# A state recurrence that takes its context as a weighted sum, and k and q projected by pairs of heads

## Chip, cores and metric

The kernel runs on one core of one Trainium2 chip. The metric is device microseconds (us) from the first to the last instruction and what lies around them; lower is better. The engines are PE (TensorE, matmuls), PEld (its weight loads), DVE (VectorE), ACT (ScalarE), POOL (GpSimd) and SP (SyncE, which here issues almost all transfers). Each engine works through its own queue in program order.

## The reference, cut to what matters

One layer on 512 latent tokens and 256 context tokens of 1024 channels. Both streams are normalised and modulated to `h` and `hc`, and one projection gives u, q, k, v and two gates. Then:

```
# S5 branch, both directions, 32 groups x 64 complex states
uc, ul = u of context, u of latents
_, h0  = scan(a, B uc)             # only the last state of the context is used
h      = scan(a, B ul, start=h0)   # h[t] = a h[t-1] + B u[t]
y      = gelu(Re(C h) + d u);  ya = y * sigmoid(y @ w_glu)
# attention branch: 4 heads, 2 x 64 dims, rope on latent q and k
q, k = rope(q), concat(k_ctx, rope(k));  yb = diff_attention(q, k, v)
x = x + g * norm(merge(ya, yb, gates) @ w_out)
x = x + g2 * norm(mixture of 16 experts (1024 -> 2048 -> 1024, float32) of norm(x))
```

The context's own output is not wanted, so only its end state h0 matters.

## The kernel before, in words

**The order of the work.** The program is one long list written out by hand, in these stages: loads, normalisation and u; the matrices of the recurrence (`matrices`, `state_make`, `cp_make`); gates 0 to 7 with the convolution taps, with the recurrence woven in; v; `readout`; the GLU and its projection; k, then q; attention with gates 8 to 15; the output projection; routing; 16 experts, whose weights (402 MB) stream in as fast as room comes free.

**The recurrence.** The 768 tokens are cut into 96 chunks of 8 (32 of context, 64 of latents). `SR` holds one complex state per chunk and direction. `scan` walks over the chunks: each step is four DVE instructions on 64 columns that multiply the last state by the eighth power of a (`AR`, `AI`, from `PW[:, :, 8]`) and add the chunk's input. `steps(n)` issues n of the 95 steps at given places: 4 after each half of a gate, 10 after each of three parts of v, and the rest before `readout`, which needs them all. PE follows the weights of a gate: a high part made on ACT (`prep_gate`) and a low part on DVE (`lo`, put off into `due` and issued by `second_parts`).

**The matrices.** `matrices` is a generator of DVE work; `ahead(n)` advances it n pieces, between the pieces of h (`h_of`) and u (`u_some`). `cp_make` follows, 20 products of 1024 columns on DVE in all, and after it the first gates' low parts.

**k, q and the ropes.** The weights of k come in four parts of 256 rows and 512 columns, all four heads in each (`fetch`, `k_some`), so no head's k is ready before the fourth part. Then `ropes` projects q head by head and turns k and q: ACT copies the product (`raw`), DVE shuffles it, POOL multiplies by the sines, DVE multiplies by the cosines and adds, ACT and DVE split the sum into a high and a low part (`k_parts`, `q_parts`; of q, one low part in two is POOL's). `scores(0)` opens attention: its maximum (`nm`) is queued on DVE behind the ropes. Gate 9 uses the same PSUM bank as gate 8 and waits for the tanh of gate 8, which is queued on ACT behind the exponentials of `scores(0)`.

**Room.** Twenty tiles of 2048 columns go round in a queue `E`: `take` pops one, `give` returns it. The twelve U tiles become six large buffers for the experts' weights, the eight L tiles stay.

Of the kernel before, what the change touches and what calls it, by code (L numbers as in the profile page):

```python
# [33 lines left out]
def layer(ctx: ExitStack, tc: tile.TileContext, A, out):  # L34
# [12 lines left out]
    ctx.enter_context(tc.manual_schedule())  # L47


    E = deque("U6 L0 U0 U7 U10 U3 U11 L1 L2 L3 L4 U8 U1 U9 U5 L5 L6 L7 U4 U2".split())  # L50
    for k in range(12):
        up.tile([128, 2048], F32, name="place", tag=f"U{k}")
    tag_of, held = {}, {}
# [186 lines left out]
    def fetch(dst, c0, p):  # L240

        DMA.dma_start(out=dst.rearrange("p (k f) -> p k f", k=2),
                      in_=w_in[256 * p:256 * p + 256, c0:c0 + 512].rearrange("(k p) f -> p k f", p=128))

    def lo(eng, o, a, hi):
        eng.tensor_tensor(o, a, hi.bitcast(F32), op=OP.subtract)  # L246

    def parts(raw, eng):
# [8 lines left out]
        return t, [v.rearrange("p (k f) -> p k f", k=2) for v in (hi_, lo_)]  # L257

    PASSES = ((0, 0), (0, 1), (1, 0))

# [249 lines left out]
    def matrices(tl):  # L510
        for par in range(2):
            V.tensor_copy(LT[64 * par:64 * par + 64].rearrange("p q d k j -> p (q d) k j"),
                          tl[64 * par:64 * par + 64, 0:256].rearrange(
                              "p (q d k r j) -> p (q d) k r j", q=4, d=2, k=2, r=2)[:, :, :, par])
        V.memset(PW[:, 0, 0], 1.0)
        V.memset(PW[:, 1, 0], 0.0)
        V.tensor_copy(PW[:, :, 1], LT[:, 0:2].rearrange("p q d k j -> p q (d k j)"))
        yield
        for n in (1, 2, 4):
            b_re = PW[:, 0, n:n + 1, :].to_broadcast([128, n, 32])  # L520
            b_im = PW[:, 1, n:n + 1, :].to_broadcast([128, n, 32])
# [18 lines left out]
        yield  # L540
        for gh in range(2):
            for dr in range(2):
                yield from state_make(dr, gh)
# [55 lines left out]
    ahead(1)  # L599
    h_of(1, 2, 2)  # L600
    ada_half(1)
    ahead(2)
    u_some(range(2), 0)
    u_some(range(2), 1)
    ada_mod(1)
    wu.append(parts(wur[2], GP))
    h_of(0, 4, 1)
    ahead(2)
# [128 lines left out]
    for dr in range(2):  # L737
        for gh in range(2):
            cp_make(dr, gh)
        second_parts()  # L740
    give(mm)
    BZ_ = take("BZ")
    BZ = BZ_.rearrange("p (r g a h) -> p r g a h", r=2, g=32, a=2)
    GP.memset(BZ_, 0.0)
# [12 lines left out]
    def rows(s):  # L757
        cb = 97 + (31 - s if s < 32 else 127 - s)
        return SR[:, s:cb + 1:cb - s]

    def scan():
        for s in range(1, 96):
            if s == 32:
                V.tensor_copy(SR[:, 97 + 96], SR[:, 97])
            h0, h1 = rows(s - 1), rows(s)
            sp = keep.tile([128, 2, 2, 16], F32, name="sp", bufs=2)
            sq = keep.tile([128, 2, 2, 16], F32, name="sq", bufs=2)
# [63 lines left out]
                    DMA.dma_start(out=MT[par][16 * s:16 * s + 16, :, 0:s], in_=KS[1][16 * par:16 * par + 16, :, 7 - s:7])  # L831

    ft = taps()
    wv = []
# [172 lines left out]
    DMA.dma_start(out=cosT, in_=A["rope_cos"])  # L1007
    DMA.dma_start(out=sinT, in_=A["rope_sin"])
    for p in range(2):
        fetch(kraw[p], 1024, p)  # L1010
    kw = []
    for n in range(8):
        pq = bank("proj")
# [2 lines left out]
        if n < 4:  # L1016
            prep_proj(n + 4, GP)
        if n in (4, 6):
            kw.append(parts(kraw[len(kw)], GP))
            fetch(kraw[len(kw) - 1], 1024, len(kw) + 1)  # L1020
    load_proj(8)
    give(*ya_, *PW_["t"])
    three[0] = False
# [28 lines left out]
    def q_parts(h, a):  # L1052
# [25 lines left out]
    wqs = []  # L1078

    def k_some(p, w, acc, hx):  # L1080
        for h in range(HEADS):
            for kt in (2 * p, 2 * p + 1):
                for n, (a, b) in enumerate(PASSES):
                    PE.matmul(acc[h], w[a][:, kt % 2, 128 * h:128 * h + 128], hx[b][kt],  # L1084
                              start=kt == 0 and n == 0, stop=kt == 7 and n == 2, skip_group_check=True)

    for p in range(4):
        t, w = kw.pop(0)
        if p < 2:
            kw.append(parts(kraw[p], GP))  # L1090
            fetch(kraw[p], 512, p)
        else:
            wqs.append(parts(kraw[p - 2], GP))
            fetch(kraw[p - 2], 512, p)
        k_some(p, w, kcc, hc)
        if p == 3:
            wqs.append(parts(kraw[0], GP))
            for h in range(HEADS):
                for _ in k_parts(h, slice(0, TC), kcc[h]):
                    pass  # L1100
        k_some(p, w, kacc, hh)
        give(t)
    give(*hc_)

    def rope_k(h):
        return rope(kacc[h], lambda a: k_parts(h, lat, a))
# [1 line left out]
    def rope_q(h):  # L1108
        pl = four[h]("q")
        for kt in range(8):  # L1110
            for n, (a, b) in enumerate(PASSES):
                PE.matmul(pl, wqs[kt // 2][1][a][:, kt % 2, 128 * h:128 * h + 128], hh[b][kt],
                          start=kt == 0 and n == 0, stop=kt == 7 and n == 2)
        return rope(pl, lambda a: q_parts(h, a))

    def ropes():

        live = []
        todo = deque(((rope_k, 0), (rope_k, 1), (rope_q, 0), (rope_k, 2), (rope_k, 3), (rope_q, 1), (rope_q, 2), (rope_q, 3)))
        while todo or live:  # L1120
            if todo:
                f, h = todo.popleft()
                live.append(f(h))
            for g in reversed(list(live)):
                if next(g, live) is live:
                    live.remove(g)
            yield

    fr = ropes()
    next(fr)  # L1130
    wqs.append(parts(kraw[1], GP))
    next(fr)
    gate_room(px_[:, 0:2048])
    load_gate(8)
    for n in range(2, 9):
        next(fr)
        if n == 4:
            prep_gate(8, GP)
        if n == 7:
            prep_gate(9, GP)  # L1140
    fq = fr
    give(*(t for t, _ in wqs))


    araw = [take("araw") for _ in range(2)]
# [737 lines left out]
```

## Time and profile before

| | |
|---|---|
| runs | 1590.41, 1594.12, 1594.39 us; median 1594.12 |
| the profiled execution | 1590.99 us, of which the span 1589.2 |
| busy share of the span | PE 87%, DVE 34%, ACT 18%, POOL 9% |
| HBM traffic | 461.66 MB read, mean 292 GB/s over the span |
| mean granted clock of TensorE | 0.954 |

Busy shares are means over unlike stages. Up to about 640 us stages are bound now by one engine, now by another; from then on the experts' weights stream in at about 427 GB/s.

### The profile page before, as it was taken

To read this page: it belongs to the slowest core of one execution; us is meant where nothing else is said; L and a number is where in the kernel's file an instruction comes from. 1 tells how busy PE (TensorE), PEld (TensorE's weight loads), DVE (VectorE), ACT (ScalarE), POOL (GpSimd) and SP (SyncE) were. 2 spreads that over 40 slices of the span, in tenths; PEclk is the share of its full clock that TensorE was granted. 3 is DMA by queue.
4 is the path that set the end of the run, shared out by engine and by line. 5 is a ranking of instruction groups with operands and counts; after the bars stand their busy time and mean duration, and the time that the engine had idled before them with its cause. 6 is when DMAs were issued, how large, how long until landed. Compare 5 with 4: busy or idle time off the path is not lost.

```text
span 1589.2 us, 17706 instructions
## 1 busy us (share of the span) xinstructions
PE 1388.3 (87%) x7230; PEld 748.7 (47%) x7230; DVE 540.4 (34%) x1373; ACT 291.7 (18%) x568; POOL 143.3 (9%) x103
## 2 busy tenths in 40 slices
PE   6996979996997896899999989879989989979875
PEld 3775757885664675434334324324324324324322
DVE  5798652267556646211102012002112112101103
ACT  3571204245433322100000000000000000000002
POOL 2100002453114200000000000000000000000003
PEclk9998989998997897899999999999999999999998
DMA  9110512222453156799999999999999999999994
GB/s 330 43 54 27 108 52 97 80 91 72 163 205 122 53 186 247 313 428 425 408 424 427 426 427 427 426 428 426 427 427 427 426 427 427 427 427 427 427 411 158
DMA packets 76737, 467.01 MB, mean 294 GB/s; under 512 B 13700, under 2 KB 33344, under 8 KB 46416
## 3 DMA queue, kind: packets, MB, share of 16 engines
q1 hardware_dynamic: 75472, 463.62, 72.5%
q10 hardware_dynamic: 768, 2.13, 0.4%
q8 instruction: 57, 0.93, 0.2%
q14 instruction: 24, 0.20, 0.0%
q0 software_dynamic: 416, 0.12, 0.0%
HBM read 461.66 MB, written 2.10 MB: 292 GB/s over the span
## 4 chain that ended last, share of the span: by engine, by line
PE 53%; DMA 23%; DVE 12%; ACT 2%; SPq 2%; issue 1%; POOL 0%; DVEq 0%; ACTq 0%
PE gu L1708 14%; DMA we<-in_w_exp_up_dram 13%; PE yd L1740 9%; DMA we<-in_w_exp_down_dram 9%; PE gat L1678 5%; PE gate L689 4%; PE sca L1752 4%; PE wo L1550 3%; PE k L1084 1%; PE proj L689 1%; PE y L907 1%; PE o L1260 1%; PE s L1222 1%; PE ada L1167 1%; PE K L812 1%
## 5 line engine op out<-in xcount | busy, mean ns | idle before, releaser
L1708 PE MATMUL gu<-we,gm 128*64 128x512 f32 x752 | 167.0, 595 | 18.2 <-DMA we<-in_w_exp_up_dram 10.3
L1708 PE MATMUL gu<-we,gf 128*64 128x512 f32 x752 | 167.9, 599 | 14.4 <-DMA we<-in_w_exp_up_dram 9.5
L1719 DVE TENSOR_TENSOR hid<-hid,gu 128x512 f32<-128x512 f32 x32 | 22.0, 688 | 461.0 <-PE gu L1708 461.0
L1740 PE MATMUL yd<-we,hid 128*64 128x512 f32 x688 | 152.3, 594 | 6.8 <-DMA we<-in_w_exp_down_dram 6.7
L689 PE MATMUL gate<-hh,wsp 128*128 128x512 f32 x384 | 99.3, 413 | 25.2 <-DVE wsp L246 12.8
L1708 PEld LDWEIGHTS gu<-we,gm 128*64 128x64 f32 x752 | 52.7, 137 | 131.0 <-issue 104.0
L1708 PEld LDWEIGHTS gu<-we,gf 128*64 128x64 f32 x752 | 53.2, 138 | 126.4 <-issue 103.3
L1793 POOL TENSOR_TENSOR fin<-facc,gf 128x256 f32<-128x256 f32 (+1 forms) x12 | 10.6, 910 | 997.9 <-DMA we<-in_w_exp_down_dram 993.7
L1740 PEld LDWEIGHTS yd<-we,hid 128*64 128x64 f32 x688 | 49.0, 137 | 102.9 <-issue 97.4
L689 PEld LDWEIGHTS gate<-hh,wsp 128*128 128x128 f32 x384 | 74.2, 199 | 42.9 <-DVE wsp L246 13.2
L1745 DVE COPY mo<-yd 64x512 f32<-64x512 f32 x15 | 10.4, 694 | 224.4 <-ACT mo L1744 224.4
L1678 PE MATMUL gat<-mo,x 128*128 128x128 f32 x512 | 76.5, 313 | 10.2 <-DVE mo L1670 10.2
L1678 PEld LDWEIGHTS gat<-mo,x 128*128 128x128 f32 x512 | 71.9, 221 | 18.3 <-issue 15.2
L1716 ACT ACTIVATE hid<-gu 128x512 f32<-128x512 f32 x32 | 19.1, 597 | 298.9 <-PE gu L1708 298.9
L1752 PE MATMUL sca<-mo,gm 128*128 128x512 f32 (+1 forms) x136 | 61.6, 591 | 4.8 <-ACT mo L1744 4.8
L1724 ACT COPY hid<-ht 128x512 f32<-128x512 f32 x16 | 9.4, 585 | 249.0 <-PE ht L1723 249.0
L1708 PE MATMUL gu<-wl,gm 128*64 128x512 f32 x208 | 48.5, 610 | 3.1 <-DMA wl<-in_w_exp_up_dram 3.1
L1744 ACT ACTIVATE mo<-yd 64x512 f32<-64x512 f32 x15 | 8.8, 589 | 215.9 <-PE yd L1740 215.9
L1550 PE MATMUL wo<-wo,mp 128*128 128x512 f32 x192 | 45.8, 394 | 2.3 <-DVE at L1410 2.3
L1757 DVE TENSOR_TENSOR facc<-facc,sca 128x512 f32<-128x512 f32 (+1 forms) x60 | 38.7, 652 | 18.8 <-PE sca L1752 18.7
L1740 PE MATMUL yd<-wl,hid 128*64 128x512 f32 x192 | 44.4, 596 | 0.0
L1752 PEld LDWEIGHTS sca<-mo,gm 128*128 128x128 f32 x136 | 21.5, 188 | 44.4 <-DVE facc L1757 23.6
(437 smaller groups left out, 1920.4 us busy)
## 6 DMA issues: line engine op xcount, KB each, us to landing
we<-in_w_exp_gate_dram SPq DMA_DIRECT2D x47, 2048.0 KB, 33.1
we<-in_w_exp_up_dram SPq DMA_DIRECT2D x47, 2048.0 KB, 29.7
we<-in_w_exp_down_dram SPq DMA_DIRECT2D x43, 2048.0 KB, 26.0
araw<-in_w_ada_dram SPq DMA_DIRECT2D x16, 1024.0 KB, 6.1
wl<-in_w_exp_gate_dram SPq DMA_DIRECT2D x8, 2048.0 KB, 29.3
wl<-in_w_exp_down_dram SPq DMA_DIRECT2D x8, 2048.0 KB, 31.3
wl<-in_w_exp_up_dram SPq DMA_DIRECT2D x8, 2048.0 KB, 26.9
wh<-in_w_exp_gate_dram SPq DMA_DIRECT2D x10, 1024.0 KB, 33.3
```

Of the source, the lines that this page charges most:

```text
L689: PE.matmul(ps, w[:, a, kt], x[b][kt], start=kt == 0 and n == 0, stop=kt == last and n == 2)
L812: PE.matmul(pkv[:, gi, j1:j1 + 7].rearrange("p t h -> p (t h)"), lh(dr, ri), CP[dr, ri][:, 128 * gp + 16 * dr:128 * gp + 16 * dr + 112], s ...
L907: PE.matmul(py[P, o0:o0 + 128], SR[P, r0:r0 + 64, ri, gp], CP[dr, ri][P, c0], start=False, stop=(dr == 1 and ri == 1), skip_group_check=True)
L1084: PE.matmul(acc[h], w[a][:, kt % 2, 128 * h:128 * h + 128], hx[b][kt], start=kt == 0 and n == 0, stop=kt == 7 and n == 2, skip_group_check ...
L1550: PE.matmul(po[j], mparts(a, kt)[:, 128 * i:128 * i + 128], wo[kt][:, D * b + 512 * j:D * b + 512 * j + 512].bitcast(F32R), start=kt == 0 ...
L1678: PE.matmul(pg, x1[i][:, nb(d)], oh[:, i].rearrange("p e s -> p (e s)"), start=i == 0, stop=i == 3)
L1708: PE.matmul(pq[b][64 * j:64 * j + 64], xst[e // 2 % 2][:, kt, e % 2], wv[:, c:c + 512], start=kt == 0, stop=kt == 7, skip_group_check=True)
L1716: S.activation(hid[0][:, 1 - e % 2, b], pq[b], AF.Silu)
L1719: V.tensor_tensor(act, act, pgu[1][b], op=OP.mult)
L1740: PE.matmul(py[64 * j:64 * j + 64], hT_[:, b, i, 64 * jf:64 * jf + 64], wv[:, c:c + 512], start=(q == 0 and i == 0), stop=(q == 3 and i == ...
L1752: PE.matmul(po, gm[:, g0:g0 + 128], yp_[:, ep % 2, c], start=True, stop=True)
L1757: V.tensor_tensor(dst, dst, po, op=OP.add)
```

## The change

**Context as a sum.** `matrices` gets six more pieces: `P8`, the powers 0 to 31 of the eighth power of a, by five complex products of 1, 2, 4, 8 and 15 powers. `context` forms the end state of the context of each direction as the sum over its 32 chunks of the chunk's input times a power: for the real and the imaginary part four products of 512 columns, one addition and one reduction of 1024 columns, all on DVE. It writes the sum into `SR`, and `scan` starts at step 32: 64 steps in place of 95.

**Where it stands.** Gates 0 and 1 have no steps beside them; after each, `second_parts` and one half of `context` follow. Gates 2 to 7 get 4 and 3 steps, each part of v gets 8. `mm` (scratch) and `P8` are given back after gate 1. The calls of `ahead` after the second half of the modulation are 4 and 1 in place of 2.

**k and q by pairs of heads.** A part of the weights is now 512 rows and 256 columns (two heads); after the second part heads 0 and 1 are complete, and their ropes run while the parts of heads 2 and 3 are projected. q of heads 0 and 1 needs only the first two parts of its weights. `launch` advances all ropes under way by one piece and starts another.

**Ropes.** The product with the sines and the second low part of q move from POOL to DVE.

**E** starts in another order.

```
@@ matrices
+        V.memset(P8[:, 0, 0], 1.0)
+        V.memset(P8[:, 1, 0], 0.0)
+        V.tensor_copy(P8[:, :, 1], PW[:, :, 8])
+        yield
+        for n in (1, 2, 4, 8, 16):
+            m = min(n, 31 - n)
...
+            cmul(V, P8[:, 0, n + 1:n + m + 1], P8[:, 1, n + 1:n + m + 1], P8[:, 0, 1:m + 1], P8[:, 1, 1:m + 1],
...
+            yield
@@ context, scan
+        for ri in range(2):
+            for d in range(2):
+                V.tensor_tensor(t[0][:, d], b[d][0], w[d][ri], op=OP.mult)
+                V.tensor_tensor(t[1][:, d], b[d][1], w[d][1 - ri], op=OP.mult)
+            V.tensor_tensor(t[0], t[0], t[1], op=OP.add if ri else OP.subtract)
+            V.tensor_reduce(ends[:, :, ri], t[0].rearrange("p d n g -> p d g n"), axis=AX.X, op=OP.add)
+            yield
+        V.tensor_copy(SR[:, 31], ends[:, 0])
+        V.tensor_copy(SR[:, 97::96], ends[:, 1:2].to_broadcast([128, 2, 2, 16]))
-        for s in range(1, 96):
-            if s == 32:
-                V.tensor_copy(SR[:, 97 + 96], SR[:, 97])
+        for s in range(32, 96):
@@ gates 0 to 7, v
-            steps(4)
-            if half == 0:
+            if n > 1:
+                steps(4 - half)
+            if half == 0 and n > 1:
                 second_parts()
...
+        if n < 2:
+            second_parts()
+            next(fctx)
+        if n == 1:
+            for _ in fctx:
+                pass
+            give(mm, P8_)
...
-        steps(5)
+        steps(8)
         second_parts()
-        steps(5)
@@ q_parts, rope
-            lo(V if c else GP, ql[h][PH[c]], a[PH[c]], qq[h][c][PH[c]])
+            lo(V, ql[h][PH[c]], a[PH[c]], qq[h][c][PH[c]])
-        GP.tensor_tensor(sw, sw, sinT, op=OP.mult)
-        yield
+        V.tensor_tensor(sw, sw, sinT, op=OP.mult)
@@ k, q
+    def launch(g):
+        advance()
+        next(g)
+        live.append(g)
...
+        k_some(p, w, kcc, hc)
+        if p % 2:
+            for h in (p - 1, p):
+                for _ in k_parts(h, slice(0, TC), kcc[h]):
+                    pass
+        if p == 3:
+            wqs.append(parts(kraw[0], GP, 4))
+        k_some(p, w, kacc, hh)
+        give(t)
+        if p % 2:
+            launch(rope_k(p - 1))
+            launch(rope_k(p))
+        else:
+            advance()
+            advance()
+    launch(rope_q(0))
+    wqs.append(parts(kraw[1], GP, 4))
     gate_room(px_[:, 0:2048])
     load_gate(8)
+    launch(rope_q(1))
+    prep_gate(8, GP)
+    launch(rope_q(2))
+    prep_gate(9, GP)
+    launch(rope_q(3))
```

## Rows read from the trace of the kernel before

**Rows 1.** The page's chain of work that ended last, shares by engine
```profile
PE 53%; DMA 23%; DVE 12%; ACT 2%; SPq 2%; issue 1%; POOL 0%; DVEq 0%; ACTq 0%
```

**Rows 2.** Busy time by stretch: us, engines' busy time, clock, DMA share, GB/s
```profile
120.00:140.00 20.00, 7.23 (x50) 5.55 (x49) 18.63 (x88) 1.54 (x2) 0.00 (x0) 0.66 0.00 1
340.00:360.00 20.00, 19.34 (x84) 15.02 (x83) 19.21 (x24) 10.98 (x18) 10.47 (x6) 1.00 0.46 151
920.00:1520.00 600.00, 541.81 (x2468) 209.87 (x2469) 86.28 (x191) 32.83 (x60) 0.00 (x0) 0.99 1.01 427
```

**Rows 3.** The chain in order of time, 130 to 235 us: start, us, what
```profile
132.80 1.23 DVE wsp L246
134.07 4.34 PE gate L689 x10
141.08 2.92 PE gate L689 x12
...
174.60 1.67 PE K L812 x16
...
196.66 4.67 DMA vraw<-in_w_in_dram
...
202.45 1.22 DVE wp L246
...
231.19 1.10 PE y L907 x16
```

**Rows 4.** One step's first instruction, L768: count, ns min/median/max, first and last start
```profile
L768 DVE TENSOR_TENSOR sp<-SR,AR x95: 218/224/342, 123.4 to 224.3; 128x64 f32<-128x64 f32 x95
```

**Rows 5.** Timeline of PE before the readout
```profile
207.22 5.60 PE L552 MATMUL v<-wp,hh 128*128 128x512 f32 x24
...
224.35 1.98 PE L907 MATMUL y<-CP,SR 64*64 64x128 f32 x16 [11.16 <-DVE SR L771]
```

**Rows 6.** Timeline of DVE, 40 to 85 us
```profile
42.58 0.29 DVE L430 TENSOR_TENSOR PW<-mm 128x128 f32<-128x128 f32 x1
...
66.48 3.17 DVE L456 TENSOR_TENSOR mm<-cn,PW 128x896 f32<-128x896 f32 x1
...
82.98 2.37 DVE L567 STREAM_TRANSPOSE u<-U 128x1024 f32<-128x1024 f32 x2 [2.79 <-ACT U L566]
```

**Rows 7.** DVE's groups, shapes apart, 334 to 371 us: count, busy us, mean ns
```profile
L1071 DVE TENSOR_TENSOR px<-px 128x512 f32<-128x512 f32 x3 | 6.9, 2312 | 0.3
L1071 DVE TENSOR_TENSOR at<-at 128x512 f32<-128x512 f32 x4 | 5.7, 1413 | 1.5 <-POOL at L1068 1.2
L1070 DVE TENSOR_TENSOR at<-at,px 128x512 f32<-128x512 f32 x4 | 5.5, 1369 | 0.0
L246 DVE TENSOR_TENSOR kq<-at,kq 64x512 fp32r<-64x512 f32 x6 | 4.1, 686 | 0.2
L1067 DVE STREAM_SHUFFLE px<-px 128x512 f32<-128x512 f32 x4 | 3.0, 738 | 0.1
...
L1070 DVE TENSOR_TENSOR px<-px 128x512 f32<-128x512 f32 x3 | 2.0, 676 | 0.0
```

**Rows 8.** Timeline of all engines, 365 to 371 us
```profile
365.29 2.50 POOL L246 TENSOR_TENSOR wsp<-px,wsp 128x1024 fp32r<-128x1024 f32 x1 [3.01 <-ACT wsp L680]
365.70 2.64 DVE L1071 TENSOR_TENSOR px<-px 128x512 f32<-128x512 f32 x1
...
370.22 0.96 DVE L1224 TENSOR_REDUCE nm<-s 128x1 f32<-128x768 f32 x1
```

**Rows 9.** Timeline of PE, 357 to 485 us
```profile
357.46 5.73 PE L689 MATMUL gate<-hh,wsp 128*128 128x512 f32 x24
375.17 5.38 PE L689 MATMUL gate<-hh,wsp 128*128 128x512 f32 x12 [11.98 <-ACT sg L703]
...
479.38 1.09 PE L1244 MATMUL pd<-ident,px 128*128 128x128 f32 x4 [1.47 <-DVE px L1237]
480.12 4.22 PE L689 MATMUL gate<-hh,wsp 128*128 128x512 f32 x12
```

More of the change, by code (lines that the diff above doesn't have):

```diff
@@ L243, in fetch, with fetch_heads, parts @@
                       in_=w_in[256 * p:256 * p + 256, c0:c0 + 512].rearrange("(k p) f -> p k f", p=128))
+    def fetch_heads(dst, c0, i):
+        DMA.dma_start(out=dst.rearrange("p (k f) -> p k f", k=4),
+                      in_=w_in[512 * (i % 2):512 * (i % 2) + 512, c0 + 256 * (i // 2):c0 + 256 * (i // 2) + 256]
+                      .rearrange("(k p) f -> p k f", p=128))
     def lo(eng, o, a, hi):
         eng.tensor_tensor(o, a, hi.bitcast(F32), op=OP.subtract)
-    def parts(raw, eng):
+    def parts(raw, eng, k=2):
         t = take("wp")
@@ L540, in matrices @@
         yield
+        V.memset(P8[:, 0, 0], 1.0)
[4 more added lines that the diff above has]
+            m = min(n, 31 - n)
+            b_re = P8[:, 0, n:n + 1, :].to_broadcast([128, m, 32])
+            b_im = P8[:, 1, n:n + 1, :].to_broadcast([128, m, 32])
+            cmul(V, P8[:, 0, n + 1:n + m + 1], P8[:, 1, n + 1:n + m + 1], P8[:, 0, 1:m + 1], P8[:, 1, 1:m + 1],
+                 b_re, b_im, *(mm[:, 1024 * i:1024 * i + 32 * m].rearrange("p (n g) -> p n g", n=m) for i in range(2)))
+            yield
         for gh in range(2):
@@ L601, in layer @@
     ada_half(1)
-    ahead(2)
+    P8_ = take("P8")
+    P8 = P8_.rearrange("p (r n g) -> p r n g", r=2, n=32)
+    ahead(4)
     u_some(range(2), 0)
@@ L605, in layer @@
     ada_mod(1)
+    ahead(1)
     wu.append(parts(wur[2], GP))
@@ L759, in rows, with context @@
         return SR[:, s:cb + 1:cb - s]
+    def context():
+        pw = [P8[:, ri].rearrange("p n (d g) -> p d n g", d=2) for ri in range(2)]
+        b = [[SR[:, 97 * d:97 * d + 32, ri] for ri in range(2)] for d in range(2)]
+        w = [[pw[ri][:, d, ::-1] if d == 0 else pw[ri][:, d] for ri in range(2)] for d in range(2)]
+        t = [mm[:, 1024 * i:1024 * i + 1024].rearrange("p (d n g) -> p d n g", d=2, n=32) for i in range(2)]
+        for ri in range(2):
[7 more added lines that the diff above has]
+        V.tensor_copy(SR[:, 97::96], ends[:, 1:2].to_broadcast([128, 2, 2, 16]))
+    ends = keep.tile([128, 2, 2, 16], F32, name="ends")
     def scan():
-        for s in range(1, 96):
-            if s == 32:
-                V.tensor_copy(SR[:, 97 + 96], SR[:, 97])
+        for s in range(32, 96):
             h0, h1 = rows(s - 1), rows(s)
@@ L1018, in layer @@
         if n in (4, 6):
-            kw.append(parts(kraw[len(kw)], GP))
-            fetch(kraw[len(kw) - 1], 1024, len(kw) + 1)
+            kw.append(parts(kraw[len(kw)], GP, 4))
+            fetch_heads(kraw[len(kw) - 1], 1024, len(kw) + 1)
     load_proj(8)
@@ L1080, in k_some, with advance @@
     def k_some(p, w, acc, hx):
-        for h in range(HEADS):
-            for kt in (2 * p, 2 * p + 1):
+        for h in (2 * (p // 2), 2 * (p // 2) + 1):
+            for k in range(4):
+                kt = 4 * (p % 2) + k
                 for n, (a, b) in enumerate(PASSES):
-                    PE.matmul(acc[h], w[a][:, kt % 2, 128 * h:128 * h + 128], hx[b][kt],
+                    PE.matmul(acc[h], w[a][:, k, 128 * (h % 2):128 * (h % 2) + 128], hx[b][kt],
                               start=kt == 0 and n == 0, stop=kt == 7 and n == 2, skip_group_check=True)
[L1087 to L1103, printed above, removed]
+    live = []
+    def advance():
+        for g in list(live):
+            if next(g, live) is live:
+                live.remove(g)
+    def launch(g):
+        advance()
+        next(g)
+        live.append(g)
     def rope_k(h):
@@ L1111, in rope_q, with ropes_left @@
             for n, (a, b) in enumerate(PASSES):
-                PE.matmul(pl, wqs[kt // 2][1][a][:, kt % 2, 128 * h:128 * h + 128], hh[b][kt],
+                PE.matmul(pl, wqs[2 * (h // 2) + kt // 4][1][a][:, kt % 4, 128 * (h % 2):128 * (h % 2) + 128], hh[b][kt],
                           start=kt == 0 and n == 0, stop=kt == 7 and n == 2)
         return rope(pl, lambda a: q_parts(h, a))
[L1116 to L1132, printed above, removed]
+    for p in range(4):
+        t, w = kw.pop(0)
+        if p < 2:
+            kw.append(parts(kraw[p], GP, 4))
+            fetch_heads(kraw[p], 512, p)
+        else:
+            wqs.append(parts(kraw[p - 2], GP, 4))
+            fetch_heads(kraw[p - 2], 512, p)
+        k_some(p, w, kcc, hc)
[10 more added lines that the diff above has]
+            launch(rope_k(p))
+        else:
+            advance()
+            advance()
+    give(*hc_)
+    launch(rope_q(0))
+    wqs.append(parts(kraw[1], GP, 4))
     gate_room(px_[:, 0:2048])
     load_gate(8)
[L1135 to L1141, printed above, removed]
-    give(*(t for t, _ in wqs))
+    launch(rope_q(1))
[3 more added lines that the diff above has]
+    launch(rope_q(3))
+    give(*(t for t, _ in wqs))
+    def ropes_left():
+        while live:
+            advance()
+            yield
+    fq = ropes_left()
     araw = [take("araw") for _ in range(2)]
```

8 lines of the change are left out of this document (4 added, 4 removed).

## The prediction

> **What bounds the kernel now.** I read four views, from far to near. First the shares of the chain that ended last: PE 53%, DMA 23%, DVE 12% [rows 1]. DVE is busy for a third of the span, yet an eighth of the chain is its own, so in some stages it is the late one. Second, the stretches show where. From 920 to 1520 us the DMA share is 1.01 at 427 GB/s: there the experts' weights set the pace, and nothing of this change works there. In 120 to 140 us DVE is busy for 18.63 of 20 us and PE for 7.23, at a mean granted clock of 0.66; in 340 to 360 us DVE is at 19.21 and POOL at 10.47 [rows 2]. Third, the chain in order of time and PE's timeline say what PE waits for. Gate 2 starts at 134.07, right behind a low part that DVE made at 132.80 [rows 3]. The readout starts at 224.35 after 11.16 us of idle PE, released by the last step of the recurrence [rows 5]. Gate 9 starts at 375.17 after 11.98 us, released by the tanh of gate 8 [rows 9]; that stood on ACT behind exponentials, which waited for the maximum that DVE began only at 370.22 [rows 8]. So PE has three holes, all made by DVE's queue. Since the weights stream into room that PE's work frees, I let all that is won before 375 us move the end by as much.
>
> **The change, part by part. Less work on DVE?** Hardly. Thirty-one steps go. Twelve steps stand between their first instruction at 123.4 and 132.80 [rows 3, 4], 0.79 us each, so 24.5 us go. In their place come the powers and the sum. A product of 128 columns takes 0.29 us, one of 512 columns 0.69 [rows 6, 7]; in proportion 32, 64, 256 and 480 columns take 0.19, 0.22, 0.42 and 0.65. Five complex products of six instructions: 6 x (0.19 + 0.22 + 0.29 + 0.42 + 0.65) = 10.6, with two memsets and a copy 10.8 us. The sum: eight products at 0.69, two additions of 1024 columns at 1.22 (as the low part at 202.45 [rows 3]), two reductions at 0.96 x 1024/768 = 1.28 [rows 8], copies 0.4: 10.9 us. DVE saves 24.5 - 21.7 = 2.8 us. What counts is where the work lies.
>
> **The powers, 54 to 95 us.** DVE has slack before the transposes at 82.98: the largest gap is the 2.79 us just before them [rows 6]. But six pieces more at the same number of `ahead` calls push three products of `state_make` behind the transposes, 3 x 1.1 us (896 columns in proportion to the 1.22) = 3.3, and from there to gate 2 I found no gap on DVE's timeline. And the product at 66.48 took 3.17 us where 1.1 is its own time [rows 6], so DVE is held up while it should catch up; with fuller queues I add 1.9. The low part for gates 0 and 1 and the products of `cp_make` are queued behind, and PE waits for both. I take 5.2 us; bounds 3.3 (the rest hidden) and 10.8 (nothing hidden).
>
> **Gate 2.** Before, twelve steps (9.35 us) stand between the last product of `cp_make` and the low part for gate 2. Now none does: it starts at 123.4 + 5.2 = 128.6 and PE's gate at 129.9, against 134.07: 4.2 us won. The sum's first half (5.4), the low part of gate 3 and the second half are queued behind; gate 3's is done at 136.6, and PE wants it at 129.9 + 11.2. From there to the end of the taps PE is the bound: 174.60 + 1.67 = 176.27 before [rows 3], 172.1 now. SP's 30 small transfers follow, then those of v's third and fourth part: 196.66 before, 192.5 now.
>
> **The readout.** By then 42 + 8 steps are issued, and DVE has had 50 us for them. What is left is a queue on DVE: v's third low part, which waits for the transfer (202.45 - 4.2 = 198.2, ending 199.5), eight steps (6.3), the fourth low part (1.2), six steps (4.7): 211.7. PE is free earlier, since v ends at 207.22 + 5.60 = 212.8 before [rows 5] and 208.6 now. So the readout starts at 211.7 against 224.35: **12.6 us**. Bounds: 2.8 (DVE the bound all the way, so that only its own saving counts) and 14.5 (only 3.3 us lost to the powers). Work moved past SP's queue costs nothing here: the loads keep their places.
>
> **k, q and the ropes.** PE's products stay as they are in number and size, so I leave gate 8 in its place (357.46 to 363.2 [rows 9]). DVE's work by head is a shuffle 0.74, three products or sums at 0.68 and two low parts at 0.69 [rows 7]: 4.2 us, where two heads' worth now runs under the projections of heads 2 and 3. Of the seven last ropes' sums and products, three groups took 10.7 us more than 11 x 0.68 [rows 7]: one began at 365.70 while POOL worked from 365.29 to 367.79 and ended 0.55 us after it [rows 8]. With the sines on DVE (8 x 0.68 + 4 x 0.69 = 8.2 us more) most of these meetings go; POOL keeps the low parts of weights. The maximum then needs the scores, which end before 357.46 (the first half about 1 us earlier, at 356.6), and behind q2's rope I allow for one meeting with POOL, 2.5 us [rows 8]: it starts at 359.1. From maximum to gate 9 it took 375.17 - 370.22 = 4.95 us; so gate 9 starts at 364.1, hardly later than gate 8 and its tanh allow (363.2 + 0.6). **11.1 us.** Bounds: 11.4, and 3 if DVE stays the late one (below). Gate 8's weights are loaded in time if q's last part, now converted behind the first q, doesn't hold them up; its wait would stand on ACT, ahead of q's copies.
>
> The Trainium skill (Perfetto Trace Analysis, Optimizing Scalar/DVE Operations) speaks against this edit: with a saturated VectorE, giving work to ScalarE or even GpSimd may make sense, and here it is taken back. The same skill (SBUF — State Buffer, Who interferes with whom) holds that a VectorE instruction with two SBUF inputs and a GpSimd instruction that reads SBUF exclude each other, the later one blocking fully, which is what the 2.64 us at 365.70 shows. By the first alone the edit costs 8.2 us, by the second it gives back more than it costs; the row decides for the second.
>
> **The clock.** After each hole PE runs slow at first: gate 2's first 10 records took 4.34 us against 2.92 for 12 [rows 3], gate 9's 12 took 5.38 [rows 9], the readout's first groups 1.98 against 1.10 [rows 3, 5]: about 1.4 + 2.5 + 2 = 5.9 us. Holes of 1 to 4 us remain, and after one of 1.47 us 12 records took 4.22 [rows 9]. Half is won: **3 us**, bounds 0 and 5.9.
>
> **Sum:** 1591.0 - 12.6 - 11.1 - 3.0 = 1564.3 us for the profiled execution. The median of the runs shown lies 3.1 us above it; I forecast 1565.
>
> **The rivals.** *DVE is the bound from 54 to 224 us* (the powers are paid in full, on a queue whose work shrinks by 2.8 us). For it: 18.63 of 20 us before 140; against it: PE alone is busy throughout 141 to 176. Readout 2.8 us early, little of the clock: 1591 - 2.8 - 11.1 - 1.5 = 1576. Chance 0.12.
>
> *DVE stays late in the ropes*: the long instructions are not POOL's doing, or the new meetings with its low parts cost as much, so that 11.1 less 8.2 = 3 us is left: 1591 - 12.6 - 3 - 1.5 = 1574. For it: 19.21 of 20 us. Chance 0.12. It is what the first page named above would give.
>
> *The change buys nothing*: the holes are filled, and the time is lost again before the experts begin, as where attention is paced by DVE's short waits. For it: 12% of the chain is DVE's in many places. Within 0.3% of 1594 us, about what a measurement of this kernel can tell from no change. Chance 0.04.
>
> *Slower: the experts' stream falters.* `E` starts in another order, so other tiles become the ring of buffers, and SP takes room strictly in order: one piece freed late holds up all behind it. The share is 1.01 now [rows 2]. Over some 890 us of streaming a loss of 3% costs the 27 us won; at 5% it is 44.5: 1564 + 44.5 = 1609. Against it: in the listing the tiles that serve the last stages before the experts stay the same in kind. Chance 0.04.
>
> **Numbers.** Forecast 0.68, its own range 1557 to 1572 (low: powers 3.3, clock in full; high: no clock, powers 8). With the two weaker cases the range is 1555 to 1579; what is left out is the same, the slower and the tails, 0.2. Faster by over 0.3%: 0.68 + 0.24 = 0.92; within 0.3%: 0.04; slower: 0.04.
>
> **What would show it.** Right: gate 2 near 130, the readout near 212 and gate 9 near 350 (364 less the readout's gain and some clock), each behind a hole of under 4 us; DVE's sums in the ropes near 0.7 us; experts' stream at 427 GB/s, begun some 26 us earlier. Wrong: the first product of `cp_make` over 8 us later than now; the readout still waiting over 6 us for the last step; ACT idle before the weights of gate 8; a DMA share under 0.98 after 920 us less the shift.

## The result, and the profile after

The changed kernel takes 1575.28 us, median of four runs (1571.01 to 1577.86), beside 1594.26 before (1590.41 to 1595.14). The ratio of the runs is 0.9883, with a 95% interval of 0.9854 to 0.9912: 1.2% faster. The forecast was 1565, its range 1555 to 1579. The profiled execution is the fastest of the four, 1571.01 us, its span 1569.2 against 1589.2: 20.0 us less.

The page's chain of waits of the changed kernel, to be set beside [rows 1]:

```profile
PE 53%; DMA 24%; DVE 9%; ACT 3%; SPq 2%; issue 1%; POOL 0%; DVEq 0%; ACTq 0%
```

DVE's share of the chain has fallen by three points, though its busy time has gone from 540.4 to 542.1 us. Busy time by stretch, with the columns of [rows 2]:

```profile
120.00:140.00 20.00, 17.03 (x111) 13.81 (x110) 19.55 (x22) 5.22 (x7) 0.56 (x1) 1.00 0.17 53
340.00:360.00 20.00, 14.59 (x54) 10.97 (x53) 14.88 (x23) 16.21 (x25) 7.16 (x3) 0.85 0.30 116
920.00:1520.00 600.00, 539.87 (x2452) 207.49 (x2452) 84.61 (x185) 32.88 (x60) 0.00 (x0) 0.99 1.01 427
```

From 120 to 140 us DVE is still full, but PE now works 17 of the 20 us. The experts' stream is at 427 GB/s as before. PE's timeline of the changed kernel, 110 to 365 us:

```profile
118.86 11.63 PE L710 MATMUL gate<-hh,wsp 128*128 128x512 f32 x50 [0.48 <-ACT SR L755]
133.46 2.56 PE L710 MATMUL gate<-hh,wsp 128*128 128x512 f32 x10 [2.97 <-DVE wsp L252]
...
210.64 0.44 PE L944 MATMUL y<-MT,u 128*64 128x128 f32 x4
212.88 1.17 PE L951 MATMUL y<-CP,SR 64*64 64x128 f32 x16 [1.80 <-DVE SR L807]
...
344.58 5.73 PE L710 MATMUL gate<-hh,wsp 128*128 128x512 f32 x24
355.72 5.33 PE L710 MATMUL gate<-hh,wsp 128*128 128x512 f32 x12 [5.41 <-ACT sg L724]
```

The reader is to compare the brackets with [rows 3, 5, 9]. The hole before gate 2 is 2.97 us and was 12.77, the one before the readout 1.80 and was 11.16, the one before gate 9 5.41 and was 11.98. But gate 2 starts only 0.6 us earlier: its work now begins late instead, since gate 0 starts at 118.86 and not at 109.64. The 20.0 us of the profiled execution are: readout 11.5 earlier; 1.0 in the readout, which took 25.6 us from first to last product and takes 24.6; 7.0 between the readout's end and gate 9, 125.2 us before (249.93 to 375.17) and 118.3 now (237.45 to 355.72); 0.5 behind that.

### The profile page after: what moved, and what is told of

Read it like the earlier page. It is cut to its first block, busy times and chain, and to the rows that moved or that the text cites. A ratio compares the mean times of both kernels' runs of the same rounds, so it can differ in the third digit from the quotient of the medians.

```text
span 1569.2 us, 17614 instructions
## 1 busy us (share of the span) xinstructions
PE 1388.5 (88%) x7230; PEld 747.5 (48%) x7230; DVE 542.1 (35%) x1307; ACT 292.5 (19%) x568; POOL 125.4 (8%) x91
## 4 chain that ended last, share of the span: by engine, by line
PE 53%; DMA 24%; DVE 9%; ACT 3%; SPq 2%; issue 1%; POOL 0%; DVEq 0%; ACTq 0%
PE gu L1761 15%; DMA we<-in_w_exp_up_dram 13%; DMA we<-in_w_exp_down_dram 10%; PE yd L1793 10%; PE gat L1731 5%; PE gate L710 4%; PE sca L1805 4%; PE wo L1603 3%; PE k L1128 1%; PE proj L710 1%; PE o L1313 1%; PE y L951 1%; PE s L1275 1%; PE ada L1220 1%; PE K L848 1%
```

## The experiments

Times of one kernel spread over some 5 us from run to run, so what separates two kernels is read from distances in the profiles. Three are enough. *Front*: from the second block of products of `ada` (at 51.2 to 52.8 us) to gate 0. *Readout*: when its first product with the states starts, from the start of the span. *Ropes*: from the readout's last product to gate 9. Each ratio is to runs of the kernel before that were made beside that kernel (their medians are 1592.8 to 1594.3 us), so it is not the quotient of two medians of the table.

```
kernel        median   ratio to before [95%]        front  readout  ropes
before        1594.26  1                             58.4   224.35  125.2
changed       1575.28  0.9883 [0.9854, 0.9912]       67.4   212.88  118.3
ctx_only      1583.58  0.9949 [0.9934, 0.9964]       70.1   217.76  125.3
kq_only       1584.98  0.9961 [0.9948, 0.9975]       58.3   224.44  118.4
sines_pool    1587.02  0.9963 [0.9952, 0.9975]       70.0   217.29  120.7
load_first    1575.51  0.9896 [0.9876, 0.9917]       70.2   218.00  118.4
no_powers     1570.57  0.9850 [0.9830, 0.9869]       62.3   212.24  118.1
half_steps    1576.58  0.9889 [0.9867, 0.9910]       70.1   216.06  118.1
powers_late   1573.29  0.9887 [0.9861, 0.9913]       62.6   216.45  118.2
lows_dve      1579.32  0.9909 [0.9889, 0.9929]       70.4   218.88  116.2
pfront        1570.35  0.9853 [0.9835, 0.9870]       58.3   214.07  118.3
early_lows    1573.13  0.9868 [0.9845, 0.9891]       70.1   217.89  113.5
both          1567.56  0.9831 [0.9812, 0.9851]       58.3   212.92  113.4
both_v        1563.17  0.9821 [0.9799, 0.9843]       58.4   208.92  113.4
```

**The halves alone.** First Context's part with the old k, q and ropes, then the other way round; one line of each edit:

```
 ctx_only: the changed kernel, with k, q and the ropes of before
-        fetch_heads(kraw[p], 1024, p)
+        fetch(kraw[p], 1024, p)
 kq_only: the kernel before, with k, q and the ropes of the changed one
-        fetch(kraw[p], 1024, p)
+        fetch_heads(kraw[p], 1024, p)
```

> Only Context's part of the recurrence is changed (powers, weighted sum, 64 steps, the order of the tiles); k, q and the ropes are as before. Theory (the change's two halves add, and what is won before the readout is carried through): the readout starts 11.5 us earlier, near 212.9, k at 286.8, and gate 9 near 362.7, 12.5 us earlier than the 375.17 of before, again behind a hole of about 12 us; the time is 12 to 13 us below before, about 1582. Rival (as predicted, the ropes are worth 11.1 us and the rest of the loss lies in the front): the time is only 9 us below before, about 1585.

> Only k, q and the ropes are changed; the recurrence has its 95 steps and the tiles their old order. Theory (the ropes' share of the 20 us is 7 to 8, the same whatever comes ahead of them): the readout starts at 224.4 as before, gate 9 near 368, 7 us earlier than before, behind a hole of about 5 us released by the tanh of gate 8, with the copy of gate 8's weights on ACT waiting for their transfer; the time is 7 to 8 us below before, about 1587. Rival (the loss of 4 us against the predicted 11.1 comes from the earlier front, which shifts POOL's low parts against DVE's products): alone, the ropes give the predicted 11 us, about 1583.

Measured: ctx_only has the ropes of before (125.3); kq_only has the front and the readout of before and the ropes of the changed kernel (118.4), with gate 9 at 368.48 behind a hole of 5.51 us, as its theory has it (its time, 1585.0, lies between theory and rival). So the ropes' 7 us are their own. The front and the readout of ctx_only are not the 67.4 and 212.88 of the changed kernel's one profile, as its theory had them, but 70.1 and 217.76, as in the other kernels below that have the powers in the front. Of the 4.9 us between the readouts 1.0 lies ahead of the front and 2.7 in it, and gate 2's first 10 products cost 1.5 (4.09 us, not 2.56), of which a little is won back; why comes below. By the ratios the halves save 0.51% and 0.39%, some 8 and 6 us; the whole saves 1.17%, which the three intervals just allow. In the profile of ctx_only gate 9 starts 7.5 us earlier than before, not 12.5, and some of that is lost again later: in the projection behind attention a group that took 5.74 us before (562.45) takes 7.37 (555.71), at a mean granted clock of 0.77 where it was 1.00. That is not the old ropes' doing: load_first below, with the new ones, shows 7.34. The time of ctx_only, 1583.6, lies between the theory's figure and the rival's, and the rival's reason fails, since the ropes alone give 7 and not 11.

**Sines back on POOL.**

```
         V.stream_shuffle(sw, raw, swap)
-        V.tensor_tensor(sw, sw, sinT, op=OP.mult)
+        GP.tensor_tensor(sw, sw, sinT, op=OP.mult)
+        yield
...
-            lo(V, ql[h][PH[c]], a[PH[c]], qq[h][c][PH[c]])
+            lo(V if c else GP, ql[h][PH[c]], a[PH[c]], qq[h][c][PH[c]])
```

> As the changed kernel, but the ropes' products with the sines and one of q's two low parts are back on POOL, each with its extra stage of the pipeline, as before the change. Theory (DVE's products of two SBUF inputs are held up while POOL reads): DVE's products and sums in the ropes show instructions of over 1.2 us again, at least six of them, and gate 9 comes 3 to 7 us later; 1578 to 1582. Rival (work given to POOL is work off a busy DVE, 8 us of it): gate 9 comes at the same time or up to 5 us earlier; 1570 to 1575.

Timeline of all engines of this kernel, from 345 us:

```profile
345.30 1.74 POOL L1112 TENSOR_TENSOR at<-at,px 128x512 f32<-128x512 f32 x1
...
345.92 1.68 DVE L1114 TENSOR_TENSOR at<-at,px 128x512 f32<-128x512 f32 x1
347.00 2.79 POOL L252 TENSOR_TENSOR wsp<-px,wsp 128x1024 fp32r<-128x1024 f32 x1
347.70 2.64 DVE L1115 TENSOR_TENSOR at<-at 128x512 f32<-128x512 f32 x1
349.76 1.71 POOL L252 TENSOR_TENSOR kq<-at,qq 64x512 fp32r<-64x512 f32 x1
...
351.53 0.94 PE L1276 MATMUL s<-kq 64*128 64x512 f32 x2 [4.47 <-POOL kq L252]
```

In both pairs shown DVE's product ends some 0.55 us behind POOL's, so that here DVE waits out the work that was given to POOL; and the scores themselves now wait 4.47 us for POOL. Six sums and products of DVE take over 1.2 us from 305 us on, as the theory has it. Gate 9's first half starts 120.7 us behind the readout, 2.4 later than in the changed kernel, and its second half, at 376.10, 134.2 (125.9 in the changed kernel): 8.3 us later. The time, 1587.0, is above the theory's 1578 to 1582. How much of the 8.3 us is the meetings, how much POOL's own lateness and how much the extra stage isn't separated.

**Load of gate 8's weights first.** In the changed kernel's timeline three things stand out between q0 and gate 9:

```profile
330.73 1.06 ACT L258 ACTIVATE wp<-px 128x1024 fp32r<-128x1024 f32 x1
...
331.87 2.75 POOL L252 TENSOR_TENSOR wp<-px,wp 128x1024 fp32r<-128x1024 f32 x1 [10.16 <-ACT wp L258]
332.29 2.88 DVE L1113 TENSOR_TENSOR at<-at,px 128x512 f32<-128x512 f32 x1
334.65 0.37 SPq L691 DMA_DIRECT2D px<-in_w_in_dram  x1
...
340.32 1.06 ACT L701 ACTIVATE wsp<-px 128x1024 fp32r<-128x1024 f32 x1 [2.49 <-DMA px<-in_w_in_dram]
341.41 1.28 ACT L1101 ACTIVATE qq<-at 64x512 fp32r<-64x512 f32 x2
...
345.79 2.40 POOL L252 TENSOR_TENSOR wsp<-px,wsp 128x1024 fp32r<-128x1024 f32 x1 [1.94 <-ACT wsp L701]
345.94 2.79 DVE L1112 TENSOR_TENSOR px<-px 128x512 f32<-128x512 f32 x1
...
350.15 0.96 DVE L1277 TENSOR_REDUCE nm<-s 128x1 f32<-128x768 f32 x1
```

DVE's products meet POOL at 332.29 and 345.94 (2.8 us each where 0.69 is their own time), and ACT waits 2.49 us for a load that goes out only at 334.65: it fills the buffer that POOL's low part at 331.87 still reads. This experiment takes away the second:

```
-    launch(rope_q(0))
     wqs.append(parts(kraw[1], GP, 4))
     gate_room(px_[:, 0:2048])
     load_gate(8)
+    launch(rope_q(0))
```

> As the changed kernel, but the last part of q's weights is converted, and the load of gate 8's weights issued, ahead of the first head of q in the order of the program instead of behind it. Theory (the ropes gave 7 and not 11 us because ACT waits at 340.32 for that load, with q0's and q1's copies queued behind): the 2.49 us of idle ACT there and the 0.31 us of PE go, gate 9 starts 1.5 to 4 us earlier than 355.72, and the time is 1.5 to 4 us below the changed kernel's, 1571 to 1574. Rival (DVE's meetings with POOL alone make the ropes late): ACT's wait goes, and gate 9 stays within 0.5 us of 355.72; 1575.

Its timeline of all engines in the same stretch:

```profile
332.06 2.77 POOL L252 TENSOR_TENSOR wp<-px,wp 128x1024 fp32r<-128x1024 f32 x1 [5.25 <-ACT wp L258]
332.49 2.89 DVE L1113 TENSOR_TENSOR px<-px 128x512 f32<-128x512 f32 x1
...
342.99 1.06 ACT L701 ACTIVATE wsp<-px 128x1024 fp32r<-128x1024 f32 x1
344.13 2.77 POOL L252 TENSOR_TENSOR wsp<-px,wsp 128x1024 fp32r<-128x1024 f32 x1 [9.31 <-ACT wsp L701]
344.56 2.88 DVE L1113 TENSOR_TENSOR at<-at,px 128x512 f32<-128x512 f32 x1
```

ACT's bracket is gone, and the ropes still take 118.4: three products of DVE now meet POOL (332.49, 344.56, 351.71). My theory alone does not hold; gate 9's distance and the time are as the rival has them.

**POOL's low parts on DVE.** Now the meetings go instead. The low part of gate 9 was put behind the exponentials, which write over the weights that it reads: in this kernel gate 9's values are not the reference's, and that part waits for them.

```
-    wqs.append(parts(kraw[1], GP, 4))
+    wqs.append(parts(kraw[1], None, 4))
+    launch(rope_q(1))
+    second_parts()
     gate_room(px_[:, 0:2048])
     load_gate(8)
-    launch(rope_q(1))
-    prep_gate(8, GP)
+    prep_gate(8, None)
     launch(rope_q(2))
-    prep_gate(9, GP)
+    second_parts()
+    prep_gate(9, None)
...
         if i == 0:
+            second_parts()
```

> As the changed kernel, but three low parts of weights that POOL makes beside the ropes (the last of q, gates 8 and 9) are made by DVE instead, each at a place where its chain waits or behind the maximum. Theory (what is missing of the ropes' 11 us are DVE's three products of 2.8 us while POOL works): no product or sum of the ropes behind q0 takes over 1.2 us, the maximum starts 2 to 4 us earlier behind the readout, gate 9 too, and the time is 2 to 4 us below the changed kernel's, 1571 to 1573. Rival (the products' wait is replaced by DVE's own low parts at 1.2 us and by the waits for their transfers): gate 9 stays within 1 us of its distance of 142.9 us from the readout; 1574 to 1577.

Two rows of its timeline, SP's queue and ACT:

```profile
341.01 0.37 SPq L691 DMA_DIRECT2D px<-in_w_in_dram  x1
...
346.78 1.06 ACT L701 ACTIVATE wsp<-px 128x1024 fp32r<-128x1024 f32 x1 [5.04 <-DMA px<-in_w_in_dram]
```

Between q0 and gate 9 the meetings are gone and the ropes take 116.2, 2.1 us less, as the theory has it; but ACT's wait for the load has grown from 2.49 to 5.04 us. The time, 1579.3, is outside both ranges; its interval overlaps that of the changed kernel. The place of gate 9's part explains some of it: the gate's second half starts at 371.19, 7.8 us later than in the changed kernel, where the readout was 6.0 later, so there the 2.1 us are lost again.

**Both at once.**

```
             launch(rope_k(p - 1))
+            if p == 3:
+                wqs.append(parts(kraw[1], None, 4))
             launch(rope_k(p))
...
-    launch(rope_q(0))
-    wqs.append(parts(kraw[1], GP, 4))
+    second_parts()
     gate_room(px_[:, 0:2048])
     load_gate(8)
+    launch(rope_q(0))
     launch(rope_q(1))
-    prep_gate(8, GP)
+    prep_gate(8, None)
     launch(rope_q(2))
+    second_parts()
-    prep_gate(9, GP)
+    prep_gate(9, None)
     launch(rope_q(3))
+    second_parts()
```

> As the changed kernel, but the last part of q's weights is converted between the ropes of k2 and k3, the load of gate 8's weights is issued right behind it, and the low parts of these and of gates 8 and 9 are made by DVE instead of POOL, behind the sums of k3, q1 and q2. Theory (two things hold the ropes up in turn, DVE's meetings with POOL and ACT's wait for gate 8's load, and either is hidden behind the other when only one goes): no product of the ropes behind k3 takes over 1.2 us, ACT does not wait for the load, and gate 9 starts 139 to 140.5 us behind the readout against 142.8 (changed kernel) and 143.0 (load ahead alone); 2 to 4 us less time than the changed kernel, 1571 to 1573. Rival (the chain of each head from ACT to DVE and back sets the pace, and neither matters): gate 9 stays within 1 us of 142.8 behind the readout; 1574 to 1577.

The same places in its timeline, and PE's gate 9:

```profile
329.13 1.23 DVE L252 TENSOR_TENSOR wp<-px,wp 128x1024 fp32r<-128x1024 f32 x1 [0.17 <-ACT wp L258]
...
330.43 0.37 SPq L691 DMA_DIRECT2D px<-in_w_in_dram  x1
...
341.53 1.06 ACT L701 ACTIVATE wsp<-px 128x1024 fp32r<-128x1024 f32 x1
...
355.99 3.02 PE L710 MATMUL gate<-hh,wsp 128*128 128x512 f32 x12 [1.10 <-ACT sg L724]
```

The load goes out 4.4 us sooner than in load_first, ACT finds it there, no product of the ropes behind k3 takes over 0.69 us, and PE's hole before gate 9 is 1.10 us; the 12 products behind it take 3.02 us and not 5.33. The ropes take 113.5, 11.8 less than before the change. It is more than the theory claimed (138.1 us from readout to gate 9, where 139 to 140.5 was expected). The two causes had stood behind each other: with one of them left, nothing (load_first) or 2.1 us (lows_dve) is gained, with both gone 4.8. The median is only 2.2 us below the changed kernel's, and the intervals overlap, so this rests on the distances.

**The powers left out.**

```
         for n in (1, 2, 4, 8, 16):
-            cmul(V, P8[:, 0, n + 1:n + m + 1], ...)
             yield
...
-        pw = [P8[:, ri].rearrange("p n (d g) -> p d n g", d=2) for ri in range(2)]
+        pw = [P8[:, ri, 1:2].to_broadcast([128, 32, 32]).rearrange("p n (d g) -> p d n g", d=2) for ri in range(2)]
```

> The 30 products that make the powers are left out: the weighted sum takes the same weight for all 32 chunks, so the recurrence's values are not the reference's; its instructions keep their number and size, and all other pieces keep their order. Theory (the powers' own time on DVE, two meetings with POOL and PE's slower clock behind the late low parts are their price): PE's hole of 3.65 us near 70 us goes, gate 0 starts near 110 to 112 against 118.9 and 122.8 in two executions with the powers, the readout near 202 to 206, and the time is 9 to 13 us below the changed kernel's, 1562 to 1566. Rival (the price is the three products of the states that went behind the transposes): gate 0 and the readout come no more than 3.5 us earlier, 1572 or more.

The powers in the changed kernel, in the timeline of DVE, POOL and PE:

```profile
56.83 2.40 POOL L252 TENSOR_TENSOR wp<-wu,wp 128x1024 fp32r<-128x1024 f32 x1 [20.88 <-ACT wp L258]
56.90 2.40 DVE L435 TENSOR_TENSOR mm<-P 128x64 f32<-128x64 f32 x1
...
66.03 2.76 POOL L252 TENSOR_TENSOR wp<-wu,wp 128x1024 fp32r<-128x1024 f32 x1 [6.80 <-ACT wp L258]
66.59 2.71 DVE L434 TENSOR_TENSOR mm<-P 128x480 f32<-128x480 f32 x1
...
72.34 2.56 PE L570 MATMUL u<-wp,hh 128*128 128x512 f32 x10 [3.65 <-DVE hh L252]
```

Two products that take 0.22 and 0.65 us by themselves take 2.40 and 2.71 beside POOL, h's low part is late, and PE waits 3.65 us. In the profile of load_first, which is the same up to there, the last row reads:

```profile
73.42 4.63 PE L570 MATMUL u<-wp,hh 128*128 128x512 f32 x10 [3.65 <-DVE hh L252]
```

The same hole, and behind it PE's clock at its lower level. So it was in all six of the other profiles with the powers there (4.63 or 4.64 us). The front shows it as 67.4 against 70.0 to 70.4. Without the powers it is 62.3, so their work costs 5.1 us, and mostly 7.7 with the clock. The theory had put more on it: gate 0 comes at 115.07, not at 110 to 112. 4 us of the front, 58.4 before against 62.3, remain, and these the rival's cause explains, the order of the pieces (the next experiment but one shows it). The readout comes at 212.24, against 218.00 in load_first, where 202 to 206 was expected, and the time, 1570.6, lies between the theory's range and the rival's.

**Half of the steps left out.**

```
-        for s in range(32, 96):
+        for s in range(64, 96):
```

> The first 32 of the 64 steps are left out, 25 us of DVE's work, so the recurrence's values are not the reference's; all else is as in the changed kernel. Theory (the recurrence no longer bounds the readout, but for its last hole of 1.8 us): the readout starts 1.8 to 2.5 us earlier beside v's last product, and the time is 1 to 4 us below the changed kernel's, 1571 to 1574. Rival (DVE bounds the stretch up to the readout): PE finishes v sooner as well and the readout comes 6 us earlier or more, 1569 or less.

PE's timelines of load_first, two rows, and of this kernel:

```profile
215.71 0.44 PE L944 MATMUL y<-MT,u 128*64 128x128 f32 x4
218.00 1.17 PE L951 MATMUL y<-CP,SR 64*64 64x128 f32 x16 [1.84 <-DVE SR L807]
...
215.69 0.44 PE L944 MATMUL y<-MT,u 128*64 128x128 f32 x4
216.06 1.17 PE L951 MATMUL y<-CP,SR 64*64 64x128 f32 x16
```

The readout starts 1.9 us earlier (216.06 to 218.00), v ends at the same time: 25 us of DVE's work less bring only the last hole. The theory holds; the median, 1576.6, doesn't show the 2 us. The 32 steps that are left run where the first 32 ran, beside gates 2 to 6 (149.8 to 179 us); those behind are gone. So the steps behind 179 us hold up nothing but the readout's start. For the stretch ahead of that the changed kernel's own timeline of PE speaks: from 133.46 to the end of v its largest hole is 0.69 us. PE is the bound there, not DVE.

**The powers late.** They go behind `cp_make`, beside gates 0 and 1:

```
         if n < 2:
             second_parts()
-            next(fctx)
+            for _ in range(3):
+                next(fp8, None)
...
+        if n == 2:
+            next(fctx)
+            second_parts()
+            for _ in fctx:
+                pass
```

> As the changed kernel, but the powers are made behind the last products of cp_make, in the stretch of gates 0 and 1, and the weighted sum follows gate 2 instead of gates 0 and 1; steps start with gate 3. Theory (DVE has slack of some 10 us between 140 and 212 and none before): gate 0 starts near 110 to 112, gate 2 near 124 to 126, v ends 8 us or more earlier, DVE is then the last one, and the readout starts 5 to 9 us earlier, near 205 to 209; 1566 to 1571. Rival (DVE bounds the whole stretch, so it is the same wherever the powers lie): the readout waits for the last step until 212 or later; 1574 to 1577.

The front is 62.6 without any powers in it, 4.2 us more than before. Two holes in PE's timeline, which the kernel before doesn't have, show where most of it lies:

```profile
96.82 1.06 PE L499 MATMUL WTt<-ident,wb 128*128 128x128 f32 x8 [2.14 <-DVE wb L466]
...
99.07 1.94 PE L499 MATMUL WTt<-ident,wb 128*128 128x128 f32 x8 [1.19 <-DVE wb L473]
```

Both end with a product of `state_make`; eleven of these stand behind the first transposes now, where eight stood before. So most of it is the order of the pieces and not that of `E`. Gate 0 comes at 114.28 and gate 2 at 128.61, both later than expected; gate 2 is 8.6 us earlier than in load_first. But the readout comes at 216.45, and neither theory nor rival has it right: PE, not the steps, ends last (v at 216.08), because the low parts stand behind the steps in DVE's queue. The time, 1573.3, lies between the two ranges. In PE's timeline it waits for one at gate 5 and for one at v:

```profile
165.65 4.08 PE L701 MATMUL gate<-hh,wsp 128*128 128x512 f32 x10 [3.55 <-DVE wsp L252]
...
190.00 4.37 PE L561 MATMUL v<-wp,hc 128*128 128x512 f32 x11 [1.65 <-DVE wp L252]
```

**The front in its old order, and the low parts ahead of the steps.** The second part of the edit, against the changed kernel:

```
-            if n > 1:
-                steps(4 - half)
+            if half == 0 and 2 < n < 7:
+                second_parts()
+            if n > 2:
+                steps(5 - half)
```

> As the kernel that makes the powers late, with two changes: the pieces of the front have again the order, and the tiles the order E, that they had before the change (nothing of the powers is left there), and up to gate 6 DVE's low part for the next gate goes ahead of the steps. Theory (the powers' price in the front is their own work, 7 to 8 us, and the shifted order of the pieces, 5 us; late, they lie in DVE's slack): gate 0 starts near 110 as before the change, gate 2 near 124, PE waits no more than 1 us for low parts up to gate 7, and the readout starts near 206 to 209; 1563 to 1567. Rival (from gate 2 on DVE is the bound, whatever its order): the readout waits for DVE until 213 or later; 1571 or more.

The front is 58.3: with the old order all is back. The readout, at 214.07, misses the 206 to 209 and is where the rival put it, but for the same reason as above, now at v: the low parts of v's first weights still stand behind the steps of gate 7, and PE waits 5.60 us for them at 187.20. Whether the order counts, which the rival denies, the last edit tests. Together with early_lows:

> The two together: the powers late with the front in its old order, and the low parts beside the ropes on DVE with the early load. Theory (the gains lie ahead of the readout and behind it, so they add): readout near 206 to 209, gate 9 139 to 140.5 us behind it; 1560 to 1564. Rival (what is won before the readout is lost again to the clock or to transfers behind it): no better than the better of the two alone by more than 1 us.

The ropes' part is all there (113.4), the readout (212.92) not, and the time, 1567.6, is 2.8 us below pfront and 5.6 below early_lows; that the gains add fully isn't shown. The last edit is one condition, `2 < n < 7` to `n > 2`:

> As the two together, but at gate 7 as well DVE's low parts, here those of v's first two parts of weights, go ahead of the steps. Theory (with the powers late, v and with it the readout were held up by these low parts, which stood behind nine steps: PE waited 5.55 us at 186.37): that wait goes, v ends near 207, and the readout starts near 208, 4 to 5.5 us earlier than 212.9; 1561 to 1564. Rival (the steps are then the last to end, since DVE has only 5 us of slack left): the readout waits for the last step until 211 or later; 1566 or more.

PE's timeline at v with the two together, and then at v and at the readout with this edit:

```profile
186.37 4.48 PE L559 MATMUL v<-wp,hc 128*128 128x512 f32 x11 [5.55 <-DVE wp L252]
...
182.46 4.38 PE L559 MATMUL v<-wp,hc 128*128 128x512 f32 x11 [1.65 <-DVE wp L252]
...
208.92 1.17 PE L960 MATMUL y<-CP,SR 64*64 64x128 f32 x16
```

The wait goes from 5.55 to 1.65 us and the readout starts 4.0 us earlier, with no wait for a step: the order counts. At 1563.17 us this is the best kernel here: 0.9821 [0.9799, 0.9843], an interval that doesn't touch that of the changed kernel, though it overlaps those of `both`, pfront and no_powers.

## Why the prediction came out as it did

The sign was right, and the median of 1575.28 us lies in the stated range. But the forecast's own mechanism was to give 1557 to 1572; the median lies above that, in the part of the range that stood for the two weaker cases, and neither of them came about as told. So it is partly luck that the range holds it. The sum was 26.7 us and the profiled execution gave 20.0. Of the signs named for "right", the readout (212.88) and the stream's 427 GB/s came; gate 2 (133.46, not near 130) and gate 9 (355.72 behind a hole of 5.41, not near 350 behind one under 4) didn't. By its own terms:

- **Powers, 5.2 (bounds 3.3 to 10.8).** Mis-sized. The first product of `cp_make` is 8.6 us late in the profiled execution, which is one of the signs that I named for "wrong". The shift of the order, put at 3.3, is 4.0 to 4.2 (no_powers, powers_late). The rest, put at 1.9, is 5.1, most of it PE's holes of 0.73 and 3.65 us before h's products: h's low parts stand behind the powers, two of which meet POOL at 2.1 us each (without the powers one such meeting stays, with a product of `state_make`). What the sum lacks altogether is the clock behind PE's new hole, 2.7 us in six profiles of seven. With it the front is 11.7 us late, beyond my upper bound. It may explain a part of the 4.3 us by which the median lies above the profiled run, whose mean granted clock was 0.961 where the other three runs had 0.950 to 0.957; that it is this hole isn't shown.
- **Gate 2, 4.2 us earlier.** 0.6, the powers' surplus. Its first 10 products take 2.56 us instead of 4.34 in this profile, but 4.04 to 4.14 in the six others with the powers in the front.
- **Readout, 12.6.** 11.5 in the profiled execution; 5.5 to 7.1 in the five other profiles with the powers in the front and all steps. The chain was as told: v, then a short wait for the last step. But v gives little of the gain: it ends at 210.64 instead of 212.75, and the rest is the hole, 11.16 us before and 1.80 now. Half_steps shows that the wait that is left is worth 1.9 us.
- **Ropes, 11.1.** Mis-sized: 7.0. Gate 8 stayed in its place, as put. I had allowed one meeting with POOL; there are two on the way to the maximum. And the condition that I had named, that q's last part doesn't hold up the load of gate 8's weights, is not met: ACT waits 2.49 us for them. With both causes taken away the same ropes give 11.8.
- **Clock, 3.** 1.0 behind the readout's start; gate 2's 1.8 us stand ahead of it and are in the readout's 11.5. None at gate 9 in this profile, where a hole of 5.41 us costs as much clock as one of 11.98 (12 products in 5.33 and 5.38 us; 4.40 to 5.44 behind holes of 5.1 to 6.1 us in six other profiles).
- **The rest.** What was won before 375 us moved the end by as much: first gather of the experts 19.6 us earlier, end 20.0.

The rivals: that DVE bounds everything from 54 to 224 us is refuted by PE's timeline from gate 2 to the end of v and by half_steps, though its half about the powers came nearly true. That DVE stays late in the ropes was to leave 3 us of them; kq_only has 6.9, and sines_pool is slower. But DVE's meetings with POOL's low parts, named there, are one of the two things that held the ropes up. The Trainium skill (Perfetto Trace Analysis, Optimizing Scalar/DVE Operations) would give some work of a saturated VectorE to ScalarE or even GpSimd, and warns that moving it between VectorE and GpSimd might not help. In sines_pool giving it to GpSimd cost 8.3 us at gate 9's second half. The Trainium skill (SBUF — State Buffer, Who interferes with whom) holds that a GpSimd instruction reading SBUF and a VectorE one with two SBUF inputs exclude each other. Every meeting shown above agrees, as 2.88 us beside a low part of 2.75. That the change buys nothing is refuted by its interval. The rival of a faltering stream is refuted by the share of 1.01 at 427 GB/s.

## What to carry to other kernels

Where an in-order queue is full, ask of each instruction what stands behind it and who waits for that: the same powers cost the front 5.1 us, and mostly 7.7, inside it and nothing behind `cp_make`, and low parts ahead of the steps were worth 4 us without any work saved. If removing one suspected wait changes nothing, don't acquit it: take away the next suspect with it, since two waits in turn can each hide behind the other. And price a new hole in PE's work with the slow products behind it, not only with its length.

## What was not expected of the hardware

- The clock behind the same hole is not the same in each execution. After 3.65 us of idle PE before the 10 products near 73 us, TensorE kept its upper level once (2.56 us, granted clock 1.00) and fell to the lower in six profiles (4.63 or 4.64 us, 0.50). That may be some of the spread of one kernel's times. The stretch in the changed kernel and in load_first, with the columns of [rows 2]:

```profile
72.30:74.90 2.60, 2.56 (x12) 2.15 (x13) 2.56 (x3) 0.00 (x0) 0.00 (x0) 1.00 0.02 6
73.40:78.10 4.70, 4.67 (x12) 3.71 (x13) 4.63 (x5) 0.00 (x0) 0.00 (x0) 0.50 0.01 3
```

- A reduction of 1024 columns that reads them out of order (`p d n g -> p d g n`) took 1.87 and 1.89 us, where 768 columns in order take 0.96 [rows 8]; in proportion 1.28 was put. The one adds and gives 32 sums, the other takes one maximum, so which of these differences costs the time isn't shown.
